# A two-layer decoder on one core: the crowded experts' loop moved, wider register loads, earlier embeddings' products, 1/rms with one tensor operand

## The chip, the cores and the metric

The kernel runs on one core of a Trainium2 chip. The metric is the device time of one execution in microseconds (us); smaller is better.

## What is computed

Two layers act on a residual stream x of 512 tokens by 1024 channels. Each layer adds a mixer (one projection, a dilated attention and a convolution module), then a mixture of 32 experts of which each token uses two, then a gated per-layer embedding p:

```python
x += W_o (sigmoid(gate_a) * A + sigmoid(gate_b) * B)          # attention A, convolution B
x += hierarchical_MoE(rms_norm(x))    # top-1 of 4 groups, then top-2 of the 8 experts in it
x += sigmoid(rms_norm(x) @ W_pg) * (p[i] @ W_pe)
# an expert: (silu(h @ Wg) * (h @ Wu)) @ Wd, inner width 512; rms_norm = t * rsqrt(mean(t*t) + eps) * g
```

A last RMS norm ends the program. All arrays are float32.

## The kernel before

The experts of a layer (`moe`, L1032) are worked through in 14 blocks (`BLK`): blocks 0 and 1 hold two experts each that are the same for every input, blocks 2 and 3 four experts with few tokens each, the other ten two each. The 28 experts of blocks 2 to 13 stand at places of a list that is sorted on the chip by crowding (`order`), so the address of their weights is a number read at run time. A step c (0 to 6, called steps one to seven) takes two blocks: for each block the products ps_g and ps_u of 32 weight halves each (`gate_up`) and the activation (`hidden`); then the down products ps_y of the two blocks of the step before (`down`), the transposition of the activations (ps_hT), the gathering of the next step's rows (ps_xg), and the combination (ps_c), which adds the results of the step before into x. After step seven the last two blocks' down products follow.

Weights come in tiles `s_w` of 128x1024 floats, 512 KB, each one transfer issued by SyncE (SP) at L252. The pool of such buffers has 45, which x, one-hot matrices, gathered rows, results and the embeddings' tiles share. `pump` (L244) is called after each consumed tile and issues further loads, in a fixed order of items, while the used buffers plus `KEEP[c]` stay under 45. SP works strictly in order; a load waits in its queue for the landing of the load eight before it.

`expert` (L257) fetches the place's number into a register of SP the first time that an expert is needed: one load of one number (L263), and two instructions that follow it. `overflow` (L1285) handles experts with more than 64 rows: a number n is read into a register on every engine and a loop (`For_i`, L1291) runs n times; for these inputs n is 0. It is called at the end of step `OVC` + 1. `load_embeddings` issues four loads for the products p @ W_pe in step `PEC`, counted from zero; `embeddings` (24 products ps_pe, half of the work) is called at the ends of steps c = PEC and PEC + 1.

`rms_of` (L385) computes 1/sqrt by a first guess from the number's bits and three Newton steps on 128x1 columns on VectorE (DVE):

```python
v.scalar_tensor_tensor(w, m, y, y, op0=OP.mult, op1=OP.mult)      # L397
v.scalar_tensor_tensor(y, w, 1.5, y, op0=OP.add, op1=OP.mult)     # L398
```

It is called for each of four groups of 128 tokens at the start, at each routing, in each gate and at the end; L428 then makes the normed rows `s_n` from x, the column and a row of gains. GpSimd (POOL) meanwhile subtracts the rounded half of mixer weights from the whole (L239, `s_lo`).

Of the kernel before, what the change touches and what calls it, by code (L numbers as in the profile page):

```python
# [13 lines left out]
OP = mybir.AluOpType  # L14
# [3 lines left out]
T, D, P = 512, 1024, 128  # L18
# [4 lines left out]
NG, NPG, NE = 4, 8, 32  # L23
# [6 lines left out]

NST, NSM = 4, 8
NDY = NE - NST
BLK = ([(2 * i, 2 * i + 1) for i in range(NST // 2)]
       + [tuple(range(NST + 4 * i, NST + 4 * i + 4)) for i in range(NSM // 4)]
       + [(i, i + 1) for i in range(NST + NSM, NE, 2)])
NB = len(BLK)

# [25 lines left out]
NCH = len(SEQ_CHUNKS)  # L63

RING = 6, 18, 28
KEEP = 3, 8, 6, 6, 6, 6, 3
LAGS = 1, 2, 1, 5
OVC = 1
PEC = 5
PGD = "pg1", "pg2", "pg3"  # L70
PGS = 1, 3, 4, 5, 7
CT, CG = 2, 4
# [91 lines left out]
class Trunk:  # L164
    def __init__(self, ctx, tc, x, pT, wd, wg, wu, wdn, sm, gains, cst, out):
# [19 lines left out]
        for l in range(self.L):  # L185
            gu = [[(l, w, s, h) for w in ("g", "u") for h in range(4) for s in b
                   if n or w == "u" or h < 4 - LATE] for n, b in enumerate(BLK)]
            dn = [[(l, "d", s, h) for h in range(4) for s in b] for b in BLK]
            seq = gu[:2] + dn[:2]
# [67 lines left out]
    def expert(self, w, l, s):  # L257

        if s < NST:
            return self.dr[w][l, s]  # L260
        r = s - NST
        if r not in self.order_v:
            self.order_v[r] = self.nc.values_load(self.order[0:1, r:r + 1], engines=[mybir.EngineType.SP],  # L263
                                                  min_val=0, max_val=NE - 1)
        return self.dr[w][l, bass.ds(self.order_v[r], 1)].rearrange("o p f -> (o p) f")

    def late_items(self):
# [117 lines left out]
    def rms_of(self, t, s0, s1, y=None):  # L385
        v = self.nc.vector
        st = self.tn(8, f"rms{t}")
        a, b, w, m = (st[:, i:i + 1] for i in range(4))
        y = st[:, 4:5] if y is None else y
        v.tensor_scalar(b, s0, 1.0 / D, EPS, op0=OP.mult, op1=OP.add)  # L390
        v.scalar_tensor_tensor(a, s1, 1.0 / D, b, op0=OP.mult, op1=OP.add)
        wi = w.bitcast(I32)
        v.tensor_scalar(wi, a.bitcast(I32), 1, None, op0=OP.logical_shift_right)
        v.tensor_scalar(m, a, -0.5, None, op0=OP.mult)
        v.tensor_scalar(y.bitcast(I32), wi, -1, 0x5F3759DF, op0=OP.mult, op1=OP.add)
        for _ in range(3):
            v.scalar_tensor_tensor(w, m, y, y, op0=OP.mult, op1=OP.mult)  # L397
            v.scalar_tensor_tensor(y, w, 1.5, y, op0=OP.add, op1=OP.mult)  # L398
        return y

    def rms(self, t, junk):
# [529 lines left out]
    def order_experts(self):  # L931
# [10 lines left out]
        for i in range(0, NE, 8):  # L942
            v.max(out=top[:, i:i + 8], in_=src)
            if i + 8 < NE:
                v.match_replace(out=rest, in_to_replace=top[:, i:i + 8], in_values=src, imm_value=-1e9)
                src = rest
        oi = self.tn(NDY, "oi", I32)
        v.tensor_copy(oi, top[:, :NDY])
        v.tensor_scalar(oi, oi, 31, None, op0=OP.bitwise_and)
# [82 lines left out]
    def moe(self, l):  # L1032
        nc = self.nc
        self.nc = Engines(self.tc, ("te",))
        v, act, pe = nc.vector, nc.scalar, self.nc.tensor
# [3 lines left out]
        def make_rows():  # L1039
            for q in self.slots + list(self.gates) + [self.rc]:  # L1040
                ps = self.ps.get(F32, "row")
                for t in range(NT):
                    pe.transpose(ps[:, t * P:(t + 1) * P], q[:, t:t + 1].to_broadcast([P, P]), self.ident)
                r_ = self.s2.get(F32, "row")
                act.activation(r_, ps, AF.Copy)
                self.ps.free()
                rows.append(r_)
# [23 lines left out]
        def scatter_hot(p):  # L1071

            col = self.cc(C_SLOT + p, 1)
            tmp = self.s2.get(F32, "oh")
            ga = self.tn(3, "ga", bufs=2)
            g_, rh[p] = self.tn(1, f"gs{p % 2}", bufs=2), self.tn(1, f"rs{p % 2}", bufs=2)
            v.tensor_scalar(tmp, rows[0], col, None, op0=OP.is_equal)
            o = self.s2.get(F32R, "OHT")
            v.scalar_tensor_tensor(o, rows[1], col, tmp, op0=OP.is_equal, op1=OP.add)
            v.scalar_tensor_tensor(tmp, o.bitcast(F32), 0.5, rows[4], op0=OP.mult, op1=OP.mult, accum_out=rh[p])  # L1080
            for i in range(2):
                v.scalar_tensor_tensor(tmp, rows[i], col, rows[2 + i], op0=OP.is_equal, op1=OP.mult,
                                       accum_out=ga[:, i:i + 1])
            v.tensor_scalar(g_, ga[:, 0:1], ga[:, 1:2], 2.0, op0=OP.add, op1=OP.mult)
            v.tensor_scalar(g_, g_, rh[p], rh[p], op0=OP.mult, op1=OP.mult)
            oht[p], gs[p] = o, g_
            self.s2.free()

        def gate_up(p, xg, w, ps, hs):
            m = P // len(BLK[p])  # L1090
            for h in hs:
                for k in range(2):
                    for i, e in enumerate(BLK[p]):
                        s = (2 * h + k) % 4 * GS + p % 2 * P + i * m
                        pe.matmul(ps[m * i:m * i + m], xg[h // 2][:, s:s + m], self.half_item((l, w, e, h), k),
                                  start=h == 0 and k == 0, stop=h == 3 and k == 1)
                for e in BLK[p]:
                    self.item_free((l, w, e, h))
                self.pump(keep=KEEP[self.c])

        def hidden(p, pg, pu):
            t = self.s2.get(F32, "h")
            act.activation(t, pg, AF.Tanh, scale=rh[p])  # L1103
            v.scalar_tensor_tensor(t, t, 1.0, pg, op0=OP.add, op1=OP.mult)  # L1104
            v.tensor_mul(t, t, pu)  # L1105
            self.ps.free(2)
            return t
# [11 lines left out]
        def down(p):  # L1119
# [3 lines left out]
            for f in range(4):  # L1123
# [4 lines left out]
                for e in BLK[p]:  # L1128
                    self.item_free((l, "d", e, f))
                self.pump(keep=KEEP[self.c])  # L1130
            self.s2.free()
# [25 lines left out]
        def restore():  # L1157

            self.x = [self.s4.get(F32, "x") for _ in range(NT)]
            for x_, hi, lo in zip(self.x, *self.nh):  # L1160
                nc.gpsimd.tensor_tensor(x_, hi.bitcast(F32), lo.bitcast(F32), op=OP.add)
# [14 lines left out]
        def load_embeddings():  # L1176
            self.pT = Rows(self.s4, 2, F32R, "pTh"), Rows(self.s4, 2, F32R, "pTl")
            for i in range(2):
                praw, a = self.s2.get(F32, "pT"), slice(i * T, (i + 1) * T)
                nc.sync.dma_start(praw, self.dr["pT"][l][:, a])  # L1180
                act.activation(self.pT[0].t[0][:, a], praw, AF.Copy)
                nc.gpsimd.tensor_tensor(self.pT[1].t[0][:, a], praw, self.pT[0].t[0][:, a].bitcast(F32), op=OP.subtract)
                self.s2.free()
            self.lim = self.pos["pe1"]
            self.look = self.ahead = 1
            self.load_chunks(self.lim)
            self.pp = []
# [11 lines left out]
        for c in range(NC2):  # L1199
            self.c = c  # L1200
            prs = 2 * c, 2 * c + 1
            if c < NC2 - 1:
                oh = self.onehots(c + 1)
            ts = []
            for p in prs:
                pg, pu = self.ps.get(F32, "g"), self.ps.get(F32, "u")
                gate_up(p, xg, "g", pg, range(4))
                gate_up(p, xg, "u", pu, range(4))
                if p == 0:
                    with self.tc.issue_after(self.last_v), self.tc.issue_after(self.last_a):  # L1210
                        self.route()
                        make_rows()
                scatter_hot(p)
                ts.append(hidden(p, pg, pu))
                if p == 2 * PEC - 2:
                    load_embeddings()
            self.s4.free(2)
            if c == 1:
                restore()
            if c:  # L1220
                for p in prs:
                    down(p - 2)
            for p, t in zip(prs, ts):
                transp(p, t)
            if c < NC2 - 1:
                xg = [self.s4.get(F32, "xg") for _ in range(2)]
                for h in range(4):
                    gather(oh, xg, h)
                self.s4.free()
                if c == NC2 - 2:  # L1230
                    self.s4.free(2 * NT)
            if c:
                combine((2 * c - 2, 2 * c - 1))
            if c == OVC:
                self.overflow(l)
            if c in (PEC, PEC + 1):
                embeddings(c - PEC)
        self.lim = self.pos["pg7"]
# [37 lines left out]
        for t in range(NT):  # L1276
            junk = self.s4.get(F32, "j")
            r = self.rms(t, junk)
# [278 lines left out]
```

## Time and profile before

| | |
|---|---|
| time, median of three runs | 1870.59 us (1869.09 to 1871.7) |
| profiled execution, own time | 1868.48 us |
| its span | 1866.7 us |
| TensorE busy | 1765.6 us (95%) |
| VectorE busy | 877.8 us (47%) |
| ScalarE busy | 545.2 us (29%) |
| GpSimd busy | 378.4 us (20%) |
| read from memory | 474.9 MB, 256 GB/s over the span |

Most instructions carry line L102, that of a helper, so the tiles tell them apart. The span runs from the first to the last instruction of the profiled execution; the time contains it and 1.8 us around it. PE is TensorE's products, DVE VectorE, ACT ScalarE, POOL GpSimd, SP the engine that issues transfers; a "q" behind a name means its queue of control instructions. Busy shares are averages over stages that differ: the mixers (two of them, up to about 400 us and from 960 to 1320) and the experts' stages read very different amounts of memory.

### The profile page before, as it was taken

How to read it: one execution, taken by the hardware profiler on the slowest of the kernel's cores; microseconds unless marked ns; L12 is line 12 of the kernel's file. 1: busy time of each engine (PE TensorE's matmuls, PEld its weight loads, DVE VectorE, ACT ScalarE, POOL GpSimd, SP SyncE). 2: the span in 40 equal slices, each digit the busy share in tenths (PEclk: the TensorE clock that was granted, in tenths of full speed). 3: DMA queues.
4: the chain of work that ended last, by engine and by line, in shares of the span. 5: the costliest groups of instructions: out<-in, count | busy, mean ns of one | idle time of the engine just before them, and what ended most of it. 6: DMA issues, size and time to landing. Idle time of an engine off the chain costs nothing. (4 is left out here: it accounts for less than half of the span.)

```text
span 1866.7 us, 24370 instructions
## 1 busy us (share of the span) xinstructions
PE 1765.6 (95%) x8324; PEld 1057.5 (57%) x8324; DVE 877.8 (47%) x2131; ACT 545.2 (29%) x1041; POOL 378.4 (20%) x203
## 2 busy tenths in 40 slices
PE   5999999999899999998989999999989999999997
PEld 4777777753153354445777777777523344355356
DVE  5587854473041334223658777536611332342236
ACT  4355443321011011104534555343201011012145
POOL 3445332400100000001344444252001000001021
PEclk9999999999999999999999999999999999999999
DMA  5211126379979999995231112454899899999931
GB/s 222 84 64 68 57 96 232 123 293 406 419 310 419 419 420 418 419 419 236 96 120 57 66 59 69 169 192 163 313 397 419 316 419 420 418 419 419 419 136 46
DMA packets 133617, 478.67 MB, mean 256 GB/s; under 512 B 14832, under 2 KB 15344, under 8 KB 133488
## 3 DMA queue, kind: packets, MB, share of 16 engines
q1 hardware_dynamic: 133488, 477.06, 65.4%
q8 instruction: 68, 1.11, 0.2%
q14 instruction: 61, 0.50, 0.1%
HBM read 474.90 MB, written 2.10 MB: 256 GB/s over the span
## 5 line engine op out<-in xcount | busy, mean ns | idle before, releaser
L239 POOL TENSOR_TENSOR s_lo<-s_raw,s_hi 128x1024 fp32r<-128x1024 f32 x114 | 272.5, 2403 | 736.4 <-ACT s_hi L234 335.9
L102 PE MATMUL ps_y<-s_w,s_hT 128*64 128x512 f32 (+1 forms) x1024 | 237.7, 600 | 16.1 <-DMA s_w<-wdn 15.7
L102 PE MATMUL ps_u<-s_w,s_xg 128*64 128x512 f32 (+1 forms) x1024 | 239.3, 595 | 12.2 <-DMA s_w<-wu 12.0
L102 PE MATMUL ps_g<-s_w,s_xg 128*64 128x512 f32 (+1 forms) x1024 | 223.4, 602 | 9.3 <-DMA s_w<-wg 4.5
L311 PE MATMUL ps_z<-s_hTl,s_hi 128*128 128x512 f32 x512 | 203.9, 398 | 0.0
L310 PE MATMUL ps_z<-s_hTh,s_hi 128*128 128x512 f32 x512 | 201.4, 393 | 0.0
L312 PE MATMUL ps_z<-s_hTh,s_lo 128*128 128x512 f32 x512 | 199.7, 390 | 0.0
L102 PEld LDWEIGHTS ps_y<-s_w,s_hT 128*64 128x64 f32 (+1 forms) x1024 | 69.5, 130 | 181.6 <-issue 109.3
L102 PEld LDWEIGHTS ps_u<-s_w,s_xg 128*64 128x64 f32 (+1 forms) x1024 | 67.7, 130 | 178.3 <-issue 117.6
L522 DVE SCALAR_TENSOR_TENSOR s_acc<-ps_z,smt,s_acc 128x511 f32<-128x511 f32 (+27 forms) x210 | 153.8, 732 | 4.2
L102 PEld LDWEIGHTS ps_g<-s_w,s_xg 128*64 128x64 f32 (+1 forms) x1024 | 65.0, 131 | 155.3 <-issue 120.9
L234 ACT ACTIVATE s_hi<-s_raw 128x1024 fp32r<-128x1024 f32 x120 | 125.6, 1056 | 8.7 <-PE ps_wo L311 5.1
L1103 ACT ACTIVATE s_h<-ps_g,rs 128x512 f32<-128x512 f32 x28 | 19.2, 687 | 335.6 <-PE ps_g L102 316.5
L1149 DVE TENSOR_TENSOR s_x<-s_x,ps_c 128x512 f32<-128x512 f32 x112 | 75.2, 685 | 76.9 <-PE ps_c L102 55.3
L1104 DVE SCALAR_TENSOR_TENSOR s_h<-s_h,ps_g 128x512 f32<-128x512 f32 x28 | 19.2, 688 | 194.9 <-ACT s_h L1103 194.9
L1114 ACT ACTIVATE s_hT<-ps_hT 128x512 f32<-128x512 f32 x28 | 15.4, 596 | 319.5 <-PE ps_hT L102 319.5
L311 PEld LDWEIGHTS ps_z<-s_hTl,s_hi 128*128 128x128 f32 x512 | 96.3, 188 | 21.3 <-issue 3.0
L310 PEld LDWEIGHTS ps_z<-s_hTh,s_hi 128*128 128x128 f32 x512 | 96.1, 188 | 21.3 <-issue 1.0
L312 PEld LDWEIGHTS ps_z<-s_hTh,s_lo 128*128 128x128 f32 x512 | 96.3, 188 | 19.0
L102 PE MATMUL ps_xg<-s_OH,s_xh 128*128 128x256 f32 x412 | 103.0, 290 | 3.7 <-DVE s_lgT L940 3.7
L102 PE MATMUL ps_xg<-s_OH,s_xl 128*128 128x256 f32 x412 | 101.7, 287 | 0.0
L1105 DVE TENSOR_TENSOR s_h<-s_h,ps_u 128x512 f32<-128x512 f32 x28 | 19.2, 687 | 155.5 <-PE ps_u L102 155.5
(275 smaller groups left out, 2830.3 us busy)
## 6 DMA issues: line engine op xcount, KB each, us to landing
s_w<-wu SPq DMA_DIRECT2D x256, 512.0 KB, 9.9
s_w<-wdn SPq DMA_DIRECT2D x256, 512.0 KB, 9.9
s_w<-wg SPq DMA_DIRECT2D x248, 512.0 KB, 9.9
s_raw<-wd SPq DMA_DIRECT2D x124, 512.0 KB, 3.3
s_w<-wg SPq DMA_DIRECT2D x16, 256.0 KB, 7.3
s_x<-x SPq DMA_DIRECT2D x4, 512.0 KB, 9.2
out<-s_n SPq DMA_DIRECT2D x8, 256.0 KB, 2.0
s_gain<-gains SPq DMA_DIRECT2D x3, 512.0 KB, 5.3
```

Of the source, the lines that this page charges most:

```text
L102: i = f(*a, **k)
L234: nc.scalar.activation(hi, raw, AF.Copy)
L239: nc.gpsimd.tensor_tensor(lo, raw, hi.bitcast(F32), op=OP.subtract)
L310: mm(out, lh, rh, start=start, stop=False)
L311: mm(out, lh, rl, start=False, stop=False)
L312: mm(out, ll, rh, start=False, stop=stop)
L522: v.scalar_tensor_tensor(o, i, w, o, op0=OP.mult, op1=OP.add)
L1103: act.activation(t, pg, AF.Tanh, scale=rh[p])
L1104: v.scalar_tensor_tensor(t, t, 1.0, pg, op0=OP.add, op1=OP.mult)
L1105: v.tensor_mul(t, t, pu)
L1114: act.activation(o, ps, AF.Copy)
L1149: v.tensor_add(xs, xs, ps)
```

## The change

Five edits. A register load takes four places at once and drops the check of the number's bounds. The loop over crowded experts is emitted between the two blocks of step three instead of at the end of step two. `KEEP` is 6 in place of 8 in step two and 9 in place of 6 in step three. The embeddings' loads are issued in step four and not five, and their two sets of products stand at the ends of steps five and six and not six and seven. In `rms_of` three `scalar_tensor_tensor` forms become `tensor_scalar`, whose further operands are pointers to one number per partition.

```diff
--- before.py
+++ after.py
@@ -30,6 +30,7 @@
 
 NST, NSM = 4, 8
 NDY = NE - NST
+LD = 4
 BLK = ([(2 * i, 2 * i + 1) for i in range(NST // 2)]
        + [tuple(range(NST + 4 * i, NST + 4 * i + 4)) for i in range(NSM // 4)]
        + [(i, i + 1) for i in range(NST + NSM, NE, 2)])
@@ -63,10 +64,10 @@
 NCH = len(SEQ_CHUNKS)
 
 RING = 6, 18, 28
-KEEP = 3, 8, 6, 6, 6, 6, 3
+KEEP = 3, 6, 9, 6, 6, 6, 3
 LAGS = 1, 2, 1, 5
-OVC = 1
-PEC = 5
+OVC = 2
+PEC = 4
 PGD = "pg1", "pg2", "pg3"
 PGS = 1, 3, 4, 5, 7
 CT, CG = 2, 4
@@ -260,8 +261,10 @@
             return self.dr[w][l, s]
         r = s - NST
         if r not in self.order_v:
-            self.order_v[r] = self.nc.values_load(self.order[0:1, r:r + 1], engines=[mybir.EngineType.SP],
-                                                  min_val=0, max_val=NE - 1)
+            _, vs = self.nc.values_load_multi_w_load_instructions(
+                self.order[0:1, r:r + LD], engines=[mybir.EngineType.SP], min_val=0, max_val=NE - 1,
+                skip_runtime_bounds_check_because="the last five bits of an integer")
+            self.order_v.update({r + i: x for i, x in enumerate(vs)})
         return self.dr[w][l, bass.ds(self.order_v[r], 1)].rearrange("o p f -> (o p) f")
 
     def late_items(self):
@@ -388,14 +391,15 @@
         a, b, w, m = (st[:, i:i + 1] for i in range(4))
         y = st[:, 4:5] if y is None else y
         v.tensor_scalar(b, s0, 1.0 / D, EPS, op0=OP.mult, op1=OP.add)
-        v.scalar_tensor_tensor(a, s1, 1.0 / D, b, op0=OP.mult, op1=OP.add)
+
+        v.tensor_scalar(a, s1, 1.0 / D, b, op0=OP.mult, op1=OP.add)
         wi = w.bitcast(I32)
         v.tensor_scalar(wi, a.bitcast(I32), 1, None, op0=OP.logical_shift_right)
         v.tensor_scalar(m, a, -0.5, None, op0=OP.mult)
         v.tensor_scalar(y.bitcast(I32), wi, -1, 0x5F3759DF, op0=OP.mult, op1=OP.add)
         for _ in range(3):
-            v.scalar_tensor_tensor(w, m, y, y, op0=OP.mult, op1=OP.mult)
-            v.scalar_tensor_tensor(y, w, 1.5, y, op0=OP.add, op1=OP.mult)
+            v.tensor_scalar(w, y, y, m, op0=OP.mult, op1=OP.mult)
+            v.tensor_scalar(y, w, 1.5, y, op0=OP.add, op1=OP.mult)
         return y
 
     def rms(self, t, junk):
@@ -1214,6 +1218,8 @@
                 ts.append(hidden(p, pg, pu))
                 if p == 2 * PEC - 2:
                     load_embeddings()
+                if p == 2 * OVC:
+                    self.overflow(l)
             self.s4.free(2)
             if c == 1:
                 restore()
@@ -1231,8 +1237,6 @@
                     self.s4.free(2 * NT)
             if c:
                 combine((2 * c - 2, 2 * c - 1))
-            if c == OVC:
-                self.overflow(l)
             if c in (PEC, PEC + 1):
                 embeddings(c - PEC)
         self.lim = self.pos["pg7"]
```

## Rows read from the trace of the kernel before

**Rows 1.** Page, part 2: traffic in 40 slices of the span

```profile
GB/s 222 84 64 68 57 96 232 123 293 406 419 310 419 419 420 418 419 419 236 96 120 57 66 59 69 169 192 163 313 397 419 316 419 420 418 419 419 419 136 46
```

**Rows 2.** TensorE's timeline, layer two: start, us, operation, tiles, [wait <- releaser]

```profile
1457.18 8.78 PE L102 MATMUL ps_g<-s_w,s_xg 128*64 128x512 f32 x32 [2.24 <-DVEq L1291]
1514.35 1.90 PE L102 MATMUL ps_y<-s_w,s_hT 128*32 128x512 f32 x10 [0.17 <-DMA s_w<-wdn]
1532.16 7.09 PE L102 MATMUL ps_g<-s_w,s_xg 128*64 128x512 f32 x32
1629.77 3.48 PE L102 MATMUL ps_y<-s_w,s_hT 128*64 128x512 f32 x10 [3.11 <-DMA s_w<-wdn]
1684.40 9.93 PE L102 MATMUL ps_y<-s_w,s_hT 128*64 128x512 f32 x42
1699.48 1.93 PE L102 MATMUL ps_y<-s_w,s_hT 128*64 128x512 f32 x6 [0.17 <-DMA s_w<-wdn]
1750.28 13.90 PE L102 MATMUL ps_y<-s_w,s_hT 128*64 128x512 f32 x64
```

**Rows 3.** Chain that ended last: start, us, engine, tile, line

```profile
1776.97 5.44 PE ps_pe L102 x24
1782.41 13.93 PE ps_y L102 x64
```

**Rows 4.** Stretches: us, busy of PE, PEld, DVE, ACT, POOL; clock, DMA share, GB/s

```profile
524.00:545.00 21.00, 18.75 (x87) 10.98 (x88) 11.46 (x25) 2.02 (x5) 0.00 (x0) 0.92 0.51 178
1312.00:1324.00 12.00, 12.00 (x56) 8.00 (x58) 10.21 (x52) 3.64 (x10) 0.00 (x0) 0.76 0.32 106
1445.00:1466.00 21.00, 18.76 (x89) 11.22 (x89) 11.46 (x24) 1.68 (x4) 0.00 (x0) 0.92 0.53 190
```

**Rows 5.** Page, part 6: issues, KB each, median us to landing

```profile
s_w<-wu SPq DMA_DIRECT2D x256, 512.0 KB, 9.9
```

**Rows 6.** Lines L263 and L1291 on SP: ns min/median/max, first to last start

```profile
L263 SPq TENSOR_LOAD <-oi x11: 263/263/272, 1314.2 to 1320.2; - x11
L1291 SPq EVENT_SEMAPHORE  x12: 28/28/5588, 1449.9 to 1456.8; - x12
```

**Rows 7.** SP's timeline: start, us, operation, tiles, number

```profile
1320.86 11.06 SPq L252 DMA_DIRECT2D s_w<-wdn  x10
1740.09 30.94 SPq L252 DMA_DIRECT2D s_w<-wdn  x25
```

**Rows 8.** VectorE's timeline at the boundary of the layers

```profile
925.65 0.15 DVE L395 TENSOR_SCALAR rms<-rms 128x1 int32<-128x1 int32 x1
925.84 1.99 DVE L397 SCALAR_TENSOR_TENSOR rms<-rms 128x1 f32<-128x1 f32 x1
947.01 0.22 DVE L397 SCALAR_TENSOR_TENSOR rms<-rms 128x1 f32<-128x1 f32 x1
947.46 2.36 DVE L397 SCALAR_TENSOR_TENSOR rms<-rms 128x1 f32<-128x1 f32 x1
949.85 2.27 DVE L398 SCALAR_TENSOR_TENSOR rms<-rms 128x1 f32<-128x1 f32 x1
```

**Rows 9.** GpSimd's timeline in the same stretch

```profile
923.00 4.82 POOL L239 TENSOR_TENSOR s_lo<-s_raw,s_hi 128x1024 fp32r<-128x1024 f32 x2 [4.34 <-DVE s_x L1415]
947.39 7.02 POOL L239 TENSOR_TENSOR s_lo<-s_raw,s_hi 128x1024 fp32r<-128x1024 f32 x3 [4.92 <-ACT s_hi L234]
```

**Rows 10.** TensorE's timeline where it waits for 1/rms

```profile
34.94 0.79 PE L311 MATMUL ps_tb<-s_lo,s_hTh 128*128 128x512 f32 x1 [5.43 <-DVE s_lo L102]
930.46 1.06 PE L416 MATMUL ps_tr<-c,s_n 128*128 128x128 f32 x8 [2.35 <-DVE s_n L428]
956.08 1.94 PE L416 MATMUL ps_tr<-c,s_n 128*128 128x128 f32 x8 [5.47 <-DVE s_n L428]
```

**Rows 11.** Lines L1085 and L652 by form: ns min/median/max

```profile
L1085 DVE TENSOR_SCALAR gs<-gs,rs x28: 269/273/276, 417.9 to 1733.9; 128x1 f32<-128x1 f32 x28
L652 DVE TENSOR_SCALAR s_S<-s_S,den x64: 276/478/2316, 80.6 to 1167.2; 128x128 f32<-128x128 f32 x16, 128x384 f32<-128x384 f32 x16, 128x256 f32<-128x256 f32 x16, 128x512 f32<-128x512 f32 x16
```

## Prediction

> **What bounds the kernel now.** I read the slices of the page first. TensorE (PE) is 95% busy over the span, which would leave little to win, but the traffic row shows two plateaus of 419 GB/s, one per layer [rows 1]: there the experts' weights stream in, and PE has no more to do than the transfers bring. Inside the plateaus PE's waits name `s_w`, a weight tile: ten short ones in the products ps_y of step three, 3.11 us in step five, three short ones at the end of step six [rows 2]. So in steps three to six the transfers set the end, and a microsecond without traffic there is a microsecond lost. Step seven differs: its 64 products run 13.90 us without a wait [rows 2], and the chain that ended last runs through ps_pe (5.44 us) and ps_y (13.93 us) behind it [rows 3]. From there PE sets the end.
>
> Two stretches per layer break the stream [rows 4]. At the stage's start 12 us move 106 GB/s, which loses 12 x (1 - 106/419) = 9.0 us. At the loop 21 us move 190 GB/s, 11.5 us lost (178 GB/s, 12.1 us in layer one). A tile of 512 KB takes 0.524 MB / 419 GB/s = 1.25 us; it lands 9.9 us after issue [rows 5], so eight are on the way.
>
> **Four places per load.** Eleven loads of one place stand ahead of the first weight tiles in SP's queue, 1314.2 to 1320.7, one per 0.59 us, of which the load itself is 0.263 [rows 6]; the first tile follows at 1320.86 [rows 7]. Three loads of four do the same. No row shows such a load. Its bounds: it costs as much as one place (0.59 us, SP free at 1316.0) or 4 x 0.59 (SP free no sooner). Nearest is the one-place row; I take 0.59 and 0.3 for each place more, 1.5 us, SP free near 1318.8: +2.0 us a layer. Before 1318 nothing is won, for there the buffers come free only with PE's products. Ends: +2.8 if it costs as one, -1.3 if all seven loads of a layer stand in front at 4 x 0.263 us and a little more (7 x 1.1 = 7.7, SP free at 1322). The Trainium skill, page "Runtime: NRT & Kernel Launch", section "Instruction fetch mechanics", speaks against this part: a register load costs about 200 ns for each register even in bulk. By it four places take an estimated 0.8 us; no row here shows a load of four.
>
> **The loop.** It runs no pass (no expert here has over 64 rows), but its entry makes SP wait up to 5.59 us for all engines [rows 6], and PE stands 2.24 us behind it; the 32 products after it take 8.78 us where a later set takes 7.09 [rows 2]. At its present place, behind the combination, no weight is consumed for some 16 us (a step later ps_y ends at 1516.2 and the next ps_g starts at 1532.16 [rows 2]), buffers run out, and SP stands in the loop when the combination frees some. Two things change. (a) At the old place: KEEP falls 8 to 6, two tiles more are on order, and the combination's four freed buffers refill at once: 5 us or so more transfer work in a stretch that lacked 11.5 to 12.1. But the two things overlap with the ramp; I leave 4.5 us lost there. (b) At the new place, between the blocks of step three, SP again waits at the entry with all weight loads of the second block queued behind it; DVE's one-hots and ACT's copies for that step wait with it. KEEP 9 leaves up to 21 tiles; by my count of buffers they have landed 2 us after PE gets there, so the traffic stops until the first issue behind the loop: wait about 2, restart 2, about 4.1 lost. That is no row, but lies between 0 (the entry waits for engines alone, and tiles are still on the way) and 12.1 (the whole of the present gap once more). Net 12.1 - 4.5 - 4.1 = 3.5 us a layer; ends -1 and +7.6 (no loss at b). PE's own 2.2 us and the slow products cost nothing at the new place: from the ps_g start at 1457.18 to the end of ps_y PE needs 8.78 + 3 x 7.09 + 13.9 = 44 us, and the step takes 59 [rows 2]; 15 us of waiting for tiles cover it, and 10 still do with the stream 5.5 earlier. Without that cover it would cost 2.2 + 1.7 = 3.9.
>
> **The embeddings.** Their two sets of 24 products (5.44 us each [rows 3]) move from the ends of steps six and seven to those of five and six. The four loads for them (1.5 MB, 3.7 us of traffic) move in SP's queue one step ahead too, past step four's and five's weight tiles; the traffic ahead of step six's last tile stays the same, so nothing is won or lost by them, nor by POOL's two subtractions, which run beside idle time. The set behind step seven, on the chain, is removed: -5.44. The set that comes behind step five lands before step six, whose ps_y, 13.9 us from 1684.40, would end at 1698.3 and ends at 1701.4 [rows 2]: 3.1 us of waiting hide it, 2.3 stick out. Net 3.2 us a layer. Without that wait all 5.44 would be given back; but a stream that is earlier keeps it, since PE's and the transfers' times move together from step three on.
>
> **The Newton steps.** In `rms_of` the forms with two tensor operands are held by POOL: at 947.46 and after, two 128x1 operations take 2.36 and 2.27 us and a third follows; the same line takes 0.22 at 947.01 [rows 8]. They end with POOL's subtractions, three in 7.02 us from 947.39 [rows 9]. The form with one tensor operand is not held: L395 takes 0.15 at 925.65, inside POOL's run from 923.00 to 927.82, and L397 right behind it 1.99 [rows 8, 9]. PE waits for this chain at three places: 5.43, 2.35 and 5.47 us [rows 10]. The form that makes `s_n` keeps its two tensors, so it still waits until the POOL operation that runs has ended. At 956.08: without the holds `s_n` is queued at 948.2, starts when POOL's first third ends (949.8), PE goes on at 951.2, 4.9 sooner. At 930.46: of 2.35 about 1.2, since `s_n` is held in place of L397. At the start, three held steps (7 us), of which one hold remains for `s_n` and one for `s_lo`: 3.5 (2.3 to 4.5). Together 9.6. Each pointer costs: two pointers 0.273 [rows 11] against 0.22 for the old L397, so 0.055 for each of seven operations, 0.39 per call. Four calls stand on the path (start, two routings, the end): -1.6. Net 8.0; range -2.5 (nothing gained, more calls on the path) to +11.
>
> The Trainium skill, page "SBUF — State Buffer", section "Who interferes with whom", agrees as far as two inputs in SBUF contend with a GpSimd operation that reads SBUF and one input does not; but it lists `tensor_scalar` among the operations that can enter a mode that takes the shared ports. The row at 925.65 is against that for 128x1.
>
> **Sum.** Per layer 2.0 + 3.5 + 3.2 = 8.7; two layers 17.4; Newton steps 8.0; 25.4 in all. The profiled execution took 1868.48 us, 1843.1 after. The median of the runs lies 2.1 above it: 1845.2.
>
> **Rivals.** A: the loop loses at its new place what it lost at the old (the entry waits until all loads on the way have landed, up to 9.9 us [rows 5]). For it: the entry has twelve semaphore waits [rows 6]. Against: the ring there is larger. Then 2 x (2.0 + 3.2) + 8.0 = 18.4, time 1852.2. Chance 0.17.
> B: hardly any gap is left (loop term 7.6): 2 x 12.8 + 8.0 = 33.6, time 1837.0. For it: the present gap is one of buffers and order, not of the wait's length. 0.13.
> C: the one-tensor form is held too. For it: L652, a `tensor_scalar`, takes up to 2316 ns [rows 11]; but its tiles are 128 wide and more. Then 17.4 - 1.6 = 15.8, time 1854.8. 0.08. [...]
> E: the load of four costs per place, and all seven stand in front: the change doesn't do what it says. 2 x (-1.3 + 3.5 + 3.2) + 8.0 = 18.8, time 1851.8. 0.05. [...]
> D, the slower one: buffers. The embeddings' tiles (two pT, two raw that become four, two results) are held a step longer beside x, one-hots and results. I count 20 of the pool's 45 left for weights at the end of steps five and six: 25 us of traffic against 16 + 5.4 us without consumption and some 3 until tiles come free and land. It decides below about 17. If nine come out of the 20, 11 tiles are 13.8 us, and with 2 us of ramp each such stretch loses 26.3 - 13.8 = 12.5. Twice that less the 5.5 gained delays the stream by 19.5. The last tile of step seven's ps_y lands 16 tiles ahead of the last of all (issued 1771.0, landed 1780.9 [rows 5, 7]), at 1760.9, and then at 1780.4; ps_y ends at 1781.3, the combination 12.8 later, the last ps_y 13.9 later at 1808 instead of 1796.3: +11.8 a layer. 2 x 11.8 - 8.0 = +15.6, time 1886.2. Against: weights, not embeddings, get what KEEP leaves. 0.05.
>
> **How the numbers follow.** The forecast has 0.52, time 1845.2. The range goes from 1832 (B with the loads at +2.8 and Newton steps at +11: 38 us) to 1862 (A and C together: 10.4 - 1.6 = 8.8). What a measurement of this kernel can tell from no change is about 0.2%, 3.7 us. Slower: D and a little for what I don't see, 0.07. Same: 0.05, from A, C and E falling together. Faster: 0.88.
>
> **What would show it.** Right: the first tile of a layer some 4.6 us behind its first register load, not 6.7; over the 21 us at the combination of step two more than 300 GB/s; a smaller dent in step three; no ps_pe between step seven's combination and the last ps_y; no 128x1 operation on L397 or L398 over 0.3 us; PE's waits of 5.43 and 5.47 down to 2 and 0.6. Wrong: SP idle over 6 us at the loop with traffic at zero (A); ps_g or ps_u of steps six and seven waiting for `s_w` (D); L397 of 2 us beside POOL (C); seven loads ahead of the first tile (E).

## The result and the profile after

The changed kernel took 1849.51 us (median of 4 runs, 1848.89 to 1854.85); the kernel before took 1870.92 beside it. The ratio is 0.9893 with a 95% interval of 0.9874 to 0.9913: faster by 1.1%, where 1845.2 was forecast. The profiled execution took 1849.56 us, 18.9 less than that of before, where 25.4 less was forecast. So the sum was 6.5 us too large, within its range.

The page of the changed kernel, first and second part: busy time of each engine, and the traffic in 40 slices.

```profile
PE 1750.0 (95%) x8324; PEld 1055.2 (57%) x8324; DVE 871.8 (47%) x2131; ACT 544.6 (29%) x1041; POOL 379.6 (21%) x203
...
GB/s 224 84 65 68 58 79 232 145 264 384 419 359 404 419 419 419 416 419 300 86 133 58 60 57 69 180 195 139 307 391 419 341 418 419 419 414 419 419 197 46
```

The plateaus stand as in [rows 1], and the notch in each (310 and 316 before) is now 359 and 341: shallower, not gone. The stretches of [rows 4] at the combination of step two and, new, at the loop between the blocks of step three (columns as there):

```profile
523.00:544.00 21.00, 21.00 (x111) 12.93 (x111) 13.00 (x29) 3.21 (x7) 0.00 (x0) 1.00 0.95 360
545.00:561.00 16.00, 11.27 (x44) 3.36 (x42) 1.21 (x4) 0.00 (x0) 0.00 (x0) 0.79 0.77 279
```

At the old place (layer one) 178 GB/s became 360. At the new place 16 us move 279 GB/s: 16 x (1 - 279/419) = 5.3 us lost. TensorE's timeline in layer two, for [rows 2]:

```profile
1464.02 9.59 PE L103 MATMUL ps_g<-s_w,s_xg 128*64 128x512 f32 x32 [4.71 <-DMA s_w<-wdn]
...
1677.05 13.90 PE L103 MATMUL ps_y<-s_w,s_hT 128*64 128x512 f32 x64
...
1739.81 13.90 PE L103 MATMUL ps_y<-s_w,s_hT 128*64 128x512 f32 x64
```

The first product behind the loop now waits 4.71 us and names a weight transfer, of a kind (`wdn`) that ps_g does not read. Step six, whose ps_y had three waits before, runs 13.90 us without one: PE is the bound there, as forecast. The chain that ended last, around the loop and at the end of the stage, for [rows 3]:

```profile
1452.99 10.45 DMA s_w<-wdn
1464.02 9.59 PE ps_g L103 x32
...
1758.16 6.87 PE ps_c L103 x29
1765.03 13.93 PE ps_y L103 x64
```

No ps_pe stands between the combination and the last ps_y any more. The register loads ([rows 6]), SP's first tiles of layer one, and SP's semaphore waits at the loop of layer two:

```profile
L264 SPq TENSOR_LOAD <-oi x14: 297/300/512, 410.6 to 1678.3; - x14
```

```profile
399.43 11.11 SPq L253 DMA_DIRECT2D s_w<-wdn  x10
```

```profile
L1295 SPq EVENT_SEMAPHORE  x12: 28/28/28, 1453.7 to 1463.6; - x12
```

A load of four takes 0.30 us, and the 14 of them (56 before) are spread over the stage; none stands ahead of the first tile.

What SP waited for in its queue while it stood at the loop of layer two, in the kernel before and in the changed one (line and what it waited for: us in total, times, longest):

```profile
SPq L1291 <- DVEq L1290: 5.6, 1, 5.6
```

```profile
SPq L1295 <- DMA s_w<-wdn: 5.9, 5, 1.2
SPq L1295 <- DMA s_w<-wu: 3.4, 2, 2.2
```

At the old place SP waited for VectorE, at the new one for the landing of seven weight tiles, one after the other, 9.3 us.

How the 18.9 us came about, read from the start of the same product in both traces (after minus before, us, negative is earlier):

| place | layer one | layer two |
|---|---|---|
| before the routing | -0.7 | -9.9 |
| products of step one | +0.6 | -9.2 |
| end of step two | +0.6 | -9.5 |
| end of step three | -2.1 | -12.6 |
| end of step five | -3.4 | -12.8 |
| end of step six | -1.0 | -10.5 |
| last ps_y | -4.8 | -17.4 |
| in the gate's products | -3.2 | -19.0 |
| after the boundary's 1/rms | -10.1 | |

Inside step five the start of the first ps_g shows +1.7 and -8.1: the four embedding loads, now a step earlier, come ahead of its tiles, and the 4 us are back at the step's end.

The granted clock moves some of this between the layers: each stage's tail has stretches in which 128x512 products take 0.63 us and not 0.39. Layer one has them in the changed kernel, layer two had them before, 1.6 us each at two places. They cancel in the sum. Without them the expert stage gains about 7.0 and 6.7 us.

```profile
877.00:889.00 12.00, 10.80 (x45) 8.56 (x46) 5.12 (x9) 7.05 (x10) 6.13 (x4) 0.86 0.26 87
```

That is layer one of the changed kernel (the clock is the third number from the end); in layer two the same products, 1787 to 1797, have a granted clock of 1.00.

At the routing of layer one the clock does not cancel. The gathering has 36 products ahead of the sort and 28 behind it in both kernels. Those of the kernel before, then those of the changed one (us, busy of PE, PEld, ACT; clock, DMA share, GB/s):

```profile
384.60:391.20 6.60, 6.46 (x36) 6.41 (x36) 0.00 (x0) 0.64 1.03 410
393.30:396.90 3.60, 3.56 (x28) 3.41 (x28) 2.30 (x6) 1.00 0.36 139
```

```profile
384.00:388.60 4.60, 4.54 (x36) 4.38 (x36) 0.00 (x0) 1.00 1.03 414
392.40:397.50 5.10, 5.04 (x28) 4.91 (x28) 2.30 (x6) 0.67 0.19 74
```

A clock of 1.00 is the upper of its two levels, 2.4 GHz; 0.64 and 0.67 are stretches partly at the lower one, 1.2 GHz. Before, the low clock fell on the first set, behind which PE waits for the sort in any case; in the changed kernel it falls on the second, which the first expert products wait for. PE was busy for 0.31 of the 3.8 us ahead of that second set.

### The profile page after: what moved, and what is told of

The parts are those of the page before. It is cut to its first block, busy times and chain, and to the rows that moved or that the text cites. A ratio compares the mean times of both kernels' runs of the same rounds, so it can differ in the third digit from the quotient of the medians.

```text
span 1847.8 us, 24216 instructions
## 1 busy us (share of the span) xinstructions
PE 1750.0 (95%) x8324; PEld 1055.2 (57%) x8324; DVE 871.8 (47%) x2131; ACT 544.6 (29%) x1041; POOL 379.6 (21%) x203
## 4 chain that ended last, share of the span: by engine, by line
PE 62%; DMA 21%; DVE 8%; issue 5%; ACT 2%; POOL 1%; SPq 0%; POOLq 0%; DVEq 0%; ACTq 0%
DMA s_w<-wdn 11%; PE ps_g L103 8%; PE ps_xg L103 6%; PE ps_u L103 6%; PE ps_z L314 5%; PE ps_z L313 5%; PE ps_z L315 5%; PE ps_y L103 5%; DMA s_w<-wu 5%; PE ps_c L103 5%; DMA s_w<-wg 3%; PE ps_tb L313 2%; PE ps_tb L314 2%; PE ps_tb L315 2%; PE ps_S L634 2%
## 5 line engine op out<-in xcount | busy, mean ns | idle before, releaser
L103 PE MATMUL ps_y<-s_w,s_hT 128*64 128x512 f32 (+1 forms) x1024 | 222.9, 601 | 10.7 <-DMA s_w<-wdn 10.4
```

Source lines behind the costliest of these rows:

```text
L103: i = f(*a, **k)
```

## The experiments

Four kernels undo one part each in the changed kernel. They are compared by their ratios to the kernel before, since they ran on another occasion than the changed kernel; that one has 0.9893 and, run a second time, 0.9910 (0.9896 to 0.9923), mean 0.9902. A ratio of 0.001 is 1.87 us, and each difference is uncertain by some 3 us, so the traces, product against product, carry the finer reading.

### The old Newton steps

```diff
-            v.tensor_scalar(w, y, y, m, op0=OP.mult, op1=OP.mult)
-            v.tensor_scalar(y, w, 1.5, y, op0=OP.add, op1=OP.mult)
+            v.scalar_tensor_tensor(w, m, y, y, op0=OP.mult, op1=OP.mult)
+            v.scalar_tensor_tensor(y, w, 1.5, y, op0=OP.add, op1=OP.mult)
```

(and the first sum likewise)

> The changed kernel with the old rms_of (two tensor operands again), nothing else undone. Theory of the prediction: the Newton steps' edit is worth 8.0 us, so this is 8.0 slower than the changed kernel (about 1857.5). Theory from the changed kernel's trace: the holds move on to s_n (2.13 to 2.77 us beside POOL in place of 1.28) and to VectorE's s_lo, so that the start gives 0.7 and not 3.5 and the boundary 6.8; with the pointers' price at the two routings the edit is worth about 5.4: about 1855. Rival C (one-tensor form held too): no difference, 1849.5.

Ratio 0.9933 (0.992 to 0.9945): 5.8 us slower than the changed kernel, where the prediction's theory had 8.0. PE's wait at the boundary is back, and so are the held operations of [rows 8]:

```profile
954.42 1.94 PE L420 MATMUL ps_tr<-c,s_n 128*128 128x128 f32 x8 [5.46 <-DVE s_n L432]
```

```profile
945.79 2.35 DVE L401 SCALAR_TENSOR_TENSOR rms<-rms 128x1 f32<-128x1 f32 x1
948.18 2.28 DVE L402 SCALAR_TENSOR_TENSOR rms<-rms 128x1 f32<-128x1 f32 x1
```

In the trace the boundary costs 6.8 us and the start 1.7, and 0.8 is taken back at each routing, where no operation of the chain is held and the pointers only cost. Rival C is out.

### The new Newton steps alone

The same edit the other way, on the kernel before.

> The kernel before with the new rms_of alone. Theory of the prediction: 8.0 us faster (ratio 0.9957). Theory from undoing it in the changed kernel: 7 to 7.5 faster (0.9962), most of it at the boundary of the layers (6.8), some 0.7 at the start. Rival C: no difference (1.000) or slower by the pointers' price, 1.6.

Ratio 0.9963 (0.995 to 0.9976): 6.9 us faster, 1.1 less than forecast, and the two directions agree within their noise. In its trace the boundary gains 6.9 us; the first products of the experts of layer one come 2.4 us later than they would. That is the loss that the table above shows at the routing, and most of it is the clock: the 28 gathering products behind the sort take 6.1 us at a granted clock of 0.51, where the kernel before has 3.6 at 1.00.

```profile
393.20:399.40 6.20, 6.11 (x28) 6.03 (x28) 2.59 (x6) 0.51 0.17 65
```

### One place per load

```diff
-            _, vs = self.nc.values_load_multi_w_load_instructions(
-                self.order[0:1, r:r + LD], engines=[mybir.EngineType.SP], min_val=0, max_val=NE - 1,
...
+            self.order_v[r] = self.nc.values_load(self.order[0:1, r:r + 1], engines=[mybir.EngineType.SP],
+                                                  min_val=0, max_val=NE - 1)
```

> The changed kernel with one place per register load, nothing else undone. Theory of the prediction: 2.0 us a layer, so 4.0 slower (about 1853.5). Theory from the changed kernel's trace: the loads of four no longer stand ahead of the first tile, which comes 3.0 us sooner in layer one, but the fifth tile waits for a free buffer as before and the stream behind it is not earlier; so no difference beyond 1 us either way (1848.5 to 1850.5). Rival E (a load of four costs as four): up to 3 faster; the trace's 0.30 us a load speaks against it.

Ratio 0.9909 (0.9895 to 0.9923), 1.3 us slower by the ratios, no difference that can be told. The traces are finer: SP's first tile of layer one is back at 402.51, and the products are 1.7 us later by step two (2.64 against an offset of 0.95 before the stage); in layer two 1.2 us by step three. But 1.2 of layer one's 1.7 arise ahead of the first expert product: the same 28 gathering products take 6.19 us here, at a granted clock of 0.51, and 5.04 in the changed kernel.

```profile
402.51 10.37 SPq L253 DMA_DIRECT2D s_w<-wdn  x10
```

```profile
393.40:399.60 6.20, 6.19 (x28) 6.03 (x28) 2.60 (x6) 0.51 0.12 46
```

So the loads of four are worth some 0.5 us in layer one and 1.2 in layer two by these traces: less than the 2.0 forecast, and little more than the nothing that I had read from the changed kernel's trace alone. There the fifth tile and all behind it stood no better to PE than before, because a loss at the routing covers the gain. The experiment undoes the width of the load and the dropped check together; no run tells them apart.

### The loop back at the end of step two

```diff
-KEEP = 3, 6, 9, 6, 6, 6, 3
+KEEP = 3, 8, 6, 6, 6, 6, 3
-                if p == 2 * OVC:
-                    self.overflow(l)
+            if c == OVC:
+                self.overflow(l)
```

> The changed kernel with the loop back at the end of step two and KEEP back to 8 and 6. Theory of the prediction: the new place is worth 3.5 us of traffic a layer, so 7.0 slower (about 1856.5). Theory from the changed kernel's trace: 12.1 and 11.5 us of traffic lost at the old place against 8.3 and 8.5 lost at both places now; part is given back by the time of step four, 2.8 and 2.5 us remain, so 5.3 slower (about 1855). Rival A (as much lost at the new place): no difference.

Ratio 0.9924 (0.9911 to 0.9937): 4.1 us slower. PE's wait and the slow products of [rows 2] are back in the old place:

```profile
1452.59 8.78 PE L103 MATMUL ps_g<-s_w,s_xg 128*64 128x512 f32 x32 [2.24 <-DVEq L1295]
```

A cleaner measure is the time between the issues of a layer's 113th and 177th weight tiles, a span that contains both places. At 419 GB/s 64 tiles take 80.1 us:

| kernel | layer one | layer two |
|---|---|---|
| before | 91.8 | 91.2 |
| changed | 89.0 | 88.3 |
| changed, loop back | 91.9 | 91.2 |
| changed, loop left out | 83.5 | 83.2 |
| changed, loop at the end | 83.8 | 84.3 |

The move is worth 2.8 and 2.9 us a layer (forecast 3.5). It contains the two changes of KEEP, which were not tried by themselves.

### No loop at all

```diff
-                if p == 2 * OVC:
-                    self.overflow(l)
```

> The changed kernel with the call of the loop over crowded experts left out (KEEP as it is). It leaves out the handling of experts with more than 64 rows, of which these inputs have none. It prices what the loop still costs at its new place. Theory of the prediction: 4.1 us of traffic a layer there (5.3 by the changed kernel's trace), and traffic sets the end of that step, so 8 to 10 us faster than the changed kernel. Rival 1, the stream stops there for want of buffers (KEEP 9) and not for the entry: 0 to 3 faster. Rival 2, PE is the bound by then and the traffic is hidden: 0 to 4 faster, with fewer waits for s_w only.

1842.46 against 1853.54 us for the changed kernel beside it: 11.1 faster. The stretch in which the changed kernel moved 279 GB/s runs at full rate, with the same KEEP:

```profile
545.00:561.00 16.00, 16.00 (x78) 5.43 (x76) 3.13 (x8) 0.69 (x1) 0.00 (x0) 1.00 1.03 419
```

So buffers are not what stops the stream there; the entry is. By the table it costs 5.5 and 5.1 us of traffic a layer at the new place, and 3.4 and 3.1 remain at the old one for want of buffers: SP, with no loop in its way, waits there until a product of the combination gives one back.

```profile
SPq L253 <- PE ps_c L103: 6.3, 1, 6.3
```

The whole is what was forecast (4.1 + 4.5 = 8.6; measured 8.9 and 8.2 above 80.1), split the other way. The cause is the one that rival A names. The last tile before the loop is issued at 1452.99 and lands 10.45 us later, at 1463.44; SP's last wait at the loop ends at 1463.6, and PE goes on at 1464.02. With the seven waits of SP shown above, the entry waits until every load on the way has landed. What was wrong in rival A was its price: it loses 5, not 12.

### The loop behind the last down products

```diff
-                if c == NC2 - 2:
-                    self.s4.free(2 * NT)
...
         down(NB - 1)
+        self.overflow(l)
+        self.s4.free(2 * NT)
```

(with KEEP 6 in step three)

> The changed kernel with the loop behind the last two blocks' down products, where all weights have landed; the eight tiles that hold the normed rows are kept until then and KEEP is 6 in step three. Theory: no weight transfer waits behind the entry, so 4.1 to 5.3 us of traffic a layer come back and PE pays its own idle time and slow products there, 3.9: 0.4 to 3 us faster. Rival: with eight buffers fewer in steps six and seven the stream starves at the ends of those steps and the kernel is slower by up to 10.

1846.41 us, 7.1 faster than the changed kernel (ratio to the kernel before 0.9871, 0.9854 to 0.9888): more than expected, since PE pays less at the new place than at the old. It waits 2.28 and 2.27 us, and the traces show 2.3 and 2.0 us lost in all. The eight buffers held longer cost nothing: no wait for `s_w` appears in steps six and seven. The entry still waits for transfers, three of the gate's weights (5.3 us in layer two), but there they do not set the pace.

```profile
865.92 0.50 PE L1150 MATMUL ps_c<-s_yh,s_OHT 128*128 128x512 f32 x1 [2.28 <-ACTq L1293]
...
1774.34 0.50 PE L1150 MATMUL ps_c<-s_yh,s_OHT 128*128 128x512 f32 x1 [2.27 <-ACTq L1293]
```

```profile
SPq L1293 <- DMA s_raw<-wd: 5.3, 3, 2.8
```

### The embeddings a step later again

```diff
-PEC = 4
+PEC = 5
```

> The changed kernel with the embeddings' loads back in step five and the products back behind steps six and seven. Theory of the prediction, which the changed kernel's trace agrees with (2.4 us given back in step six, 5.4 won behind step seven): 3.2 us a layer, 6.4 slower (about 1856). Rival D (buffers): no difference or faster. If the shift of 5.44 us were hidden wholly or not at all: 10.9 slower or no difference.

Ratio 0.9931 (0.9918 to 0.9944): 5.4 us slower. Product against product it is 3.0 and 3.2 us a layer, the forecast's 3.2; step six waits for tiles again, and ps_pe is back on the chain.

```profile
1689.30 1.93 PE L103 MATMUL ps_y<-s_w,s_hT 128*64 128x512 f32 x6 [0.18 <-DMA s_w<-wdn]
```

```profile
1765.31 5.44 PE ps_pe L103 x24
1770.75 13.94 PE ps_y L103 x64
```

Rival D falls with this, and with the 13.90 us of step six's ps_y in the changed kernel.

### GpSimd's subtractions in halves

```diff
-                nc.gpsimd.tensor_tensor(lo, raw, hi.bitcast(F32), op=OP.subtract)
+                for a in (slice(0, T), slice(T, 2 * T)):
+                    nc.gpsimd.tensor_tensor(lo[:, a], raw[:, a], hi[:, a].bitcast(F32), op=OP.subtract)
```

In the changed kernel:

> The changed kernel with each of GpSimd's 128x1024 subtractions (L240, 2.4 us) cut into two of 128x512 (1.3 us each). Theory: VectorE's operations with two tensors (s_n, s_lo) are held until the running GpSimd operation ends, so the holds that are left halve: s_n 1.5 to 2 instead of 2.1 to 2.8 and the wait of 2.25 us at the start falls by about 1: 1 to 3 us faster. Rival: a hold goes on over both halves, since the second is queued: no difference, or up to 2 slower by GpSimd's two starts for one.

1844.98 against 1853.54 us: 8.6 faster, three times the expectation. The holds halve as expected (the same waits are 2.25 and 2.19 in the changed kernel):

```profile
33.64 0.50 PE L315 MATMUL ps_tb<-s_lo,s_hTh 128*128 128x512 f32 x1 [1.06 <-DVE s_lo L103]
...
920.97 1.06 PE L421 MATMUL ps_tr<-c,s_n 128*128 128x128 f32 x8 [0.97 <-DVE s_n L433]
```

What I had left out is the attention, where a `tensor_scalar` on tiles 128 to 512 wide (L652 in [rows 11]) is held too. Line L656 of the changed kernel, the same line of this one, and under each how long PE waited for it:

```profile
L656 DVE TENSOR_SCALAR s_S<-s_S,den x64: 275/477/2316, 79.5 to 1156.8; 128x128 f32<-128x128 f32 x16, 128x384 f32<-128x384 f32 x16, 128x256 f32<-128x256 f32 x16, 128x512 f32<-128x512 f32 x16
...
  PE ps_PT L668: 3.0, 4
```

```profile
L657 DVE TENSOR_SCALAR s_S<-s_S,den x64: 275/478/1334, 77.1 to 1150.8; 128x128 f32<-128x128 f32 x16, 128x384 f32<-128x384 f32 x16, 128x256 f32<-128x256 f32 x16, 128x512 f32<-128x512 f32 x16
...
  PE ps_PT L669: 0.3, 2
```

Its longest operation falls from 2316 to 1334 ns, PE's waits from 3.0 to 0.3 us. A further gain stands at the start (2.8 us). Of the rest, 0.5 us at the routing of layer one and 1.7 at that of layer two are the clock, which falls on the gathering ahead of the sort here and on the 28 products behind it in the changed kernel. In layer two these take 6.05 us there and 3.59 here:

```profile
1302.30:1308.40 6.10, 6.05 (x28) 5.96 (x28) 2.59 (x6) 0.52 0.13 49
```

```profile
1297.30:1301.00 3.70, 3.59 (x28) 3.42 (x28) 2.29 (x6) 1.00 0.06 24
```

No run shows that the shorter operations caused this, so of the 7.7 us between the two profiled executions some 5.5 can be put down to shorter holds.

And in the kernel before, with the old Newton steps:

> The kernel before, old rms_of, with GpSimd's subtractions in halves alone. Theory (a two-tensor operation of VectorE waits until the running GpSimd operation ends): each hold of 2.3 us becomes 1.2 or less, so the boundary's chain of three falls from 6.9 to about 3.5 and the start gains 2 to 3; with what halves gave in the mixers of the changed kernel, 7 to 12 us faster. Rival (VectorE waits for GpSimd's queue to be empty): no difference.

Ratio 0.9963 (0.995 to 0.9976): 7.0 us faster, at the lower end of the expectation. The waits there shrink less than by half, 5.47 to 4.18 at the boundary and 5.43 to 4.95 at the start: a chain of held operations meets each half anew. The longest operation of L398 (L397 of before) takes 1306 ns and not 2400. So VectorE waits for the running operation and not for GpSimd's queue, and shorter GpSimd operations do not replace the edit of the Newton steps.

```profile
955.25 1.94 PE L417 MATMUL ps_tr<-c,s_n 128*128 128x128 f32 x8 [4.18 <-DVE s_n L429]
```

```profile
L397 DVE SCALAR_TENSOR_TENSOR rms<-rms x48: 210/219/2400, 909.6 to 1861.9; 128x1 f32<-128x1 f32 x48
```

```profile
L398 DVE SCALAR_TENSOR_TENSOR rms<-rms x48: 208/219/1306, 910.3 to 1857.1; 128x1 f32<-128x1 f32 x48
```

(the kernel before, then this one)

### Both together

> The changed kernel with the loop behind the last down products (7.1 us faster than the changed kernel in the set before) and GpSimd's subtractions in halves (8.6 faster). The two act in different stages, so the theory is that they add: about 15.7 faster than the changed kernel, a ratio near 0.983 to the kernel before. Rival: the loop's wait at its new place grows, since GpSimd's subtractions for the gate follow it: 12 faster or less.

1839.43 us (1837.22 to 1839.69), ratio 0.9823 (0.9811 to 0.9836) to the kernel before. Against 0.9902 for the changed kernel that is 14.8 us faster (16.3 against its second run, 0.9910, from which the 15.7 expected were taken); the two gains add. This version beats both kernels.

## Why the prediction was right, and where its sum was too large

**Embeddings.** Right in each step: 3.1 us hidden, 2.3 given back in step six (-3.4 to -1.0 and -12.8 to -10.5 in the table: 2.4 and 2.3), 5.4 won behind step seven. Forecast 6.4 for both layers (5.44 less 2.3 is 3.1 a layer, the sum has 3.2), measured 6.2.

**The loop.** Right in kind and nearly in size: 5.7 us for both layers where 7.0 was forecast. The two halves of the step were each off. At the old place KEEP 6 and the loop's absence together close more of the gap than I left (3.4 and 3.1 lost, not 4.5); at the new place the entry costs more (5.5 and 5.1, not 4.1), since it waits for seven tiles, of which the last was issued 10.45 us before it landed, and not for 2 us of remainder. My price came from a count of buffers, and buffers do not stop the stream there. PE's own 4.71 us and its slow products (9.59 us for 32) are hidden by the transfers as said.

**Four places per load.** The step that failed is where they stand. I put three loads of 1.5 us in front; there are none, and one takes 0.30 us. So the first tile came 3.0 us sooner in layer one, as by the far end of the range, but that end was priced too high: the fifth tile waits for PE's first products as it did, and the stream gains some 0.5 us in layer one and 1.2 in layer two, not 2.0 to 2.8. By the Trainium skill, page "Runtime: NRT & Kernel Launch", section "Instruction fetch mechanics", four registers would take an estimated 0.8 us; the trace has 0.30 for four and 0.263 for one, so here the measurement decides for the change.

**The Newton steps.** The mechanism was right: no 128x1 operation of the chain is held any more, and the pointers cost what was worked out for a call. VectorE's lines L401 and L402 (L397 and L398 of before) in the changed kernel:

```profile
L401 DVE TENSOR_SCALAR rms<-rms x48: 261/272/274, 905.3 to 1842.8; 128x1 f32<-128x1 f32 x48
L402 DVE TENSOR_SCALAR rms<-rms x48: 203/212/215, 905.6 to 1843.1; 128x1 f32<-128x1 f32 x48
```

The boundary gained 6.8 us where 6.1 was forecast. Its waits, for [rows 10], and the start's:

```profile
947.58 1.06 PE L420 MATMUL ps_tr<-c,s_n 128*128 128x128 f32 x8 [0.27 <-DVE s_n L432]
```

```profile
34.87 0.50 PE L314 MATMUL ps_tb<-s_lo,s_hTh 128*128 128x512 f32 x1 [2.25 <-DVE s_lo L103]
```

The term of the start is the mis-sized one: 0.7 us where 3.5 less the pointers was forecast. The wait fell from 5.43 to 2.25, but PE comes to it 3.1 us later and goes on at 34.87, where it went on at 34.94 before. VectorE's timeline at the start:

```profile
15.34 2.13 DVE L103 SCALAR_TENSOR_TENSOR s_n<-s_x,rms,s_gain 128x1024 f32<-128x1024 f32 x1
...
29.29 2.77 DVE L103 SCALAR_TENSOR_TENSOR s_n<-s_x,rms,s_gain 128x1024 f32<-128x1024 f32 x1
31.99 2.83 DVE L103 TENSOR_TENSOR s_lo<-s_raw,s_hi 128x512 fp32r<-128x512 f32 x1
```

The pointers make the second group's chain later, its `s_n` (1.28 us before) now meets a POOL operation and takes 2.13, and PE's second group starts 1.7 us later; another part of the gain goes to `s_lo`, held for 2.83 us where 0.68 is its own time. A hold taken from one operation is handed to the next one with two tensors. The Trainium skill, page "SBUF — State Buffer", section "Who interferes with whom", tells this rightly on both counts: two inputs in SBUF contend with GpSimd, and a `tensor_scalar` can. The wide ones of L656 do, up to 2316 ns; those of 128x1 never took over 276 ns here.

**What was missed.** At each routing 1.3 and 0.8 us were lost where 0.4 was reckoned. The sum had one call of `rms_of` on the path at a routing; the products' starts shift by 0.4 us twice there, in both layers, so two of the four calls are on it, 0.8. The rest, in layer one, is the granted clock: PE's first gathered product behind the sort starts 0.9 us sooner than before, at 392.46, but the first ps_g 0.6 later, at 397.47, for the same 28 products take 5.0 us at a clock of 0.67 and took 3.6 at 1.00. The prediction had no term for the clock, and what moves its low stretch from one set of products to the other was not tried.

So of the 6.5 us that the sum was too large, some 2.4 lie at the start, 1.3 in the loop, 2.2 in the register loads (by what is left of the stage's 7.0 and 6.7 us beside the loop and the embeddings) and 1.3 at the routings, less the 0.7 that the boundary gave more than forecast; the rest is below what the traces tell.

## What to carry to other kernels

A runtime loop that runs no pass still emptied the transfer queue here: its entry waited for every load on the way, so it belongs where no transfer sets the pace (7 us here), and not merely where an engine has slack. A VectorE operation that waits for GpSimd is helped by shorter GpSimd operations as well as by one operand fewer; look through the whole kernel for rows whose longest time ends with a GpSimd operation, since a hold removed at one place moves to the next one in line. When a queue's head is cleared, ask what the fifth entry waits for before counting the time of the first. Before a difference of a microsecond or two between two traces is put down to an edit, compare the granted clock of the products in between.

## What the chip showed that I had not expected

A register load of four places takes 0.30 us, of one 0.263. The loop's entry holds SP until the landing of the last load, 10.45 us after its issue. Cutting 114 GpSimd operations of 2.42 us into 228 of 1.32 adds 20 us of GpSimd's time, and the kernel is 8.6 us faster, some 5.5 us of it by shorter holds. A `tensor_scalar` of 128x1 was never held by a GpSimd operation, one of 128x256 was, up to 2316 ns.
